# A two-layer attention encoder: swapped rotary halves by DMA, a sink column in the scores, and another order of output tiles

## The chip, the cores and the metric

The kernel runs on one core of one Trainium2 chip. A core has TensorE (PE, which multiplies matrices into PSUM), VectorE (DVE), ScalarE (ACT), GpSimd (POOL) and SyncE (SP, which here issues every DMA). The engines run at once, each through its own list of instructions in a fixed order, and wait for each other by semaphores. The metric is the time of one execution on the device in microseconds (us).

## The reference: what is computed

An input of 1024 tokens by 1024 features passes two layers and a last RMS normalisation. All is float32.

```python
def even_layer(x, mem_n, table, norm_g, w_in, sink, q_norm, k_norm, w_mem_kv, w_out):
    h = rmsnorm(x, norm_g)
    aq, ak, av, bq, bk, bv, xq, gate = _split(h @ w_in, EVEN_SPLITS)
    y_a = windowed_gqa_sink(heads(aq, A_HEADS), heads(ak, A_KV_HEADS), heads(av, A_KV_HEADS), sink, table)
    cos, sin = axial_rope_tables(S)
    qb = apply_axial_rope(rmsnorm(heads(bq, B_HEADS), q_norm), cos, sin)
    kb = apply_axial_rope(rmsnorm(heads(bk, B_KV_HEADS), k_norm), cos, sin)
    y_b = dense_gqa_blocked(qb, kb, heads(bv, B_KV_HEADS))
    y_x = memory_cross_attention(heads(xq, X_HEADS), mem_n, w_mem_kv)
    y = jnp.concatenate([...y_a, y_b, y_x...], axis=-1) * jax.nn.silu(gate)
    return x + y @ w_out
```

Group A (6 heads of 64) looks at a band of 128 keys to each side. Its softmax has one column more than it has keys, the head's sink logit, which takes a share of the sum and has no value: `softmax(concatenate([logits, sink_col]))[..., :-1]`. Group B (6 heads) looks at all 1024 keys; its queries and keys are normalised by head and rotated: each pair of quarters (x1, x2) becomes (x1 cos - x2 sin, x1 sin + x2 cos). Group X attends to 256 memory tokens. Layer 1 has a differential attention (two softmaxes, one subtracted) in place of A and B, and the same cross-attention, gate and output projection.

## The kernel before, in words

**Precision and matmuls.** Every float32 product is made of three TensorE products: both factors are split in a rounded part and a remainder (suffixes h and l, by a cast and a subtraction), and hi*hi, hi*lo and lo*hi are added up in PSUM (lines 297 and 660).

**Jobs and steps.** A layer is a list of steps (one block of 128 queries, or two, of one head) and a list of jobs (one projection of 128 features for 1024 tokens, in two halves of 512 tokens). `run_steps` emits step by step: the scores of step i and its softmax (`s1`, `finish`), the copy of the finished probabilities into a float32r tile `er` by DMA (`hop`, lines 523 to 529), some steps later their transposes through TensorE (`s2`, line 540) and the products with the values (`s3`). Between them `jobs.pull` emits groups of eight products of the job that is due, so that TensorE has other work while softmaxes run. A scheduler then puts the instructions of each engine in their final order by its own estimate of the times; an edit in one place therefore moves instructions in many others.

**PSUM.** There are two tiles of 1024 columns (tag S, for scores, and for most tiles of the output projection), two of 512 (tag A: `acc` of the projections, `ox`, `ob`, `oa` of the value products, `pre`) and two of 512 (tag T, for transposes). A tile is given out again when what reads it is done.

**The rotated projections** (`rope_job`, bq0 to bq2 and bk, each in two halves). ACT squares `acc` into `sq` (line 778), writes `qg`, scaled by the gain (779), and the two swapped halves of `rot` straight from `acc` (781). DVE multiplies `qg` by cosT and `rot` by sinT (783, 784). One group of eight products later `d1` sums the squares by TensorE (791), makes the variance (794) and adds `qg` and `rot` (796). Features are stored so that the two partners of a rotation lie 64 partitions apart. These jobs run among the eight X steps and the first B steps, from about 90 us on.

**A and B steps** of layer 0 are mixed in the order BBABBABBABBABBAA. A B step takes the row minimum of the negated scores (DVE, 1059), multiplies it by the query's scale (`mr`, DVE, 1063) and takes the exponential with its row sum on ACT (1064). An A step treats two query blocks: DVE adds bias and mask and takes the minimum, with the sink as start value (1132); ACT takes the exponential (1136) and that of the sink (`es`, 1139); DVE adds it to the sum (1141) and takes the reciprocal (1143); POOL scales (1149).

**The output projection** (`out_proj`, once a layer) treats eight tiles of 128 tokens in the order `ORD`. Some tiles had their first 4 or 6 of 8 rounds done before, as fillers (`PRE`: in layer 0 tiles 2 to 5 four rounds, 6 and 7 six; in layer 1 tiles 2, 3 and 4 six). A round is three products for each of two column halves. Tiles 0 and 1 begin with their first 6 (layer 1: 7) rounds, before the last gate is ready. After a tile's products DVE adds the residual (1274), ACT squares and sums (1275), DVE and POOL make the scale (1283, 229), DVE scales (1295), and in layer 0 TensorE transposes the tile (344) for layer 1's projections, one tile behind. `pieces` chooses the PSUM tiles: all but the last take an S tile, and the last two A tiles (in layer 1 one A tile and pieces).

Of the kernel before, what the change touches and what calls it, by code (L numbers as in the profile page):

```python
# [13 lines left out]
F32R = mybir.dt.float32r  # L14
# [18 lines left out]
FAST = ("m0", "m1", "m2", "m3")  # L33
ORD = ((0, 1, 2, 3, 4, 5, 6, 7), (0, 1, 4, 2, 5, 3, 6, 7))
JORD = "xq0 m0 g6 m1 m2 g7 m3 bk bq0 bv bq1 g3 bq2 ak av aq0 g0 aq1 g4 g1 aq2 g5 g2".split()
# [120 lines left out]
def encoder_kernel(ctx, tc, A):  # L156
# [615 lines left out]
    def rope_job(p, dst):  # L772
        gcol = gq if p is not None else small[:, C_KN:C_KN + 1]

        def consume(c0, n, acc):
# [4 lines left out]
            for a, b in ((slice(0, 64), slice(64, 128)), (slice(64, 128), slice(0, 64))):  # L780
                nc.scalar.activation(rot[a, :], acc[b, :], AF.Identity, scale=gcol[b, :])
            cs = slice(c0, c0 + 512)
            nc.vector.tensor_tensor(out=qg, in0=qg, in1=cosT[:, cs], op=ALU.mult)
            nc.vector.tensor_tensor(out=rot, in0=rot, in1=sinT[:, cs], op=ALU.mult)
            st = {}

            def d1():
                T = ps_t("ssq")
                with after_fill():
                    for i in range(4):  # L790
# [3 lines left out]
                nc.vector.tensor_scalar(out=v, in0=T[:, 0:8], scalar1=1.0 / 64, scalar2=EPS,  # L794
                                        op0=ALU.mult, op1=ALU.add)
                nc.vector.tensor_tensor(out=qg, in0=qg, in1=rot, op=ALU.add)
                if p is not None:
# [236 lines left out]
    if True:  # L1034
        def b_step(h, qb):
# [8 lines left out]
            def s1(h=h, qb=qb, e=e):  # L1044
# [17 lines left out]
                mr = stat("mr")  # L1062
                nc.vector.tensor_tensor(out=mr, in0=mn, in1=rq[:, qb, h:h + 1], op=ALU.mult)  # L1063
                nc.scalar.activation(et, Sp, AF.Exp, bias=mr, scale=nrq[:, qb, h:h + 1], accum_out=z)  # L1064
# [44 lines left out]
    if True:  # L1109
        def a_step(h, p):  # L1110
# [5 lines left out]
            def s1(h=h, p=p, e=e):  # L1116
# [5 lines left out]
                Sp = ps_s("sa").rearrange("p (j c) -> p j c", j=2)  # L1122
                et = new_e(M)[:, :768].rearrange("p (j c) -> p j c", j=2)
                mn = stat("mn2", 2)
                z = stat("z2", 2)
                for j in range(2):
                    qb = 2 * p + j
                    lo, hi = max(0, qb - 1) * P, min(8, qb + 2) * P
                    c = lo - (qb - 1) * P
                    n = hi - lo  # L1130
                    qk(Sp[:, j, c:c + n], Aq[h], qb * P, Ak["k"][h // 3], Ak["kl"][h // 3], lo, n)
                    nc.vector.tensor_tensor_reduce(out=et[:, j, c:c + n], in0=Sp[:, j, c:c + n],
                                                   in1=abias[h][:, c:c + n], scale=1.0,
                                                   scalar=nsink[:, h:h + 1], op0=ALU.add, op1=ALU.min,
                                                   accum_out=mn[:, j:j + 1])
                    nc.scalar.activation(et[:, j, c:c + n], et[:, j, c:c + n], AF.Exp,
                                         bias=mn[:, j:j + 1], scale=-1.0, accum_out=z[:, j:j + 1])
                es = stat("es", 2)
                nc.scalar.activation(es, mn, AF.Exp, bias=sinkb[:, h:h + 1], scale=1.0)
                def finish():  # L1140
                    nc.vector.tensor_tensor(out=z, in0=z, in1=es, op=ALU.add)
                    rz = stat("rz2", 2)
# [11 lines left out]
            def hop(p=p, e=e):  # L1154
                t = M.at.tile([P, 1024], F32R, tag="er", name="er", bufs=M.cfg["er"])[:, :768]
                a, b = (P if p == 0 else 0), (768 - P if p == 3 else 768)
                ef = e[0].rearrange("p j c -> p (j c)")
# [58 lines left out]
    def out_proj(l, hT_next, stack):  # L1216
# [12 lines left out]

        def pieces(i):  # L1230
            if i < TT - 1:
                S2 = ps_s("po")
# [355 lines left out]
```

## Time and profile before

| | |
|---|---|
| median of 3 runs | 1253.75 us (1253.59 to 1255.1) |
| the profiled execution | 1255.58 us |
| its span, first to last instruction | 1253.8 us |
| mean granted TensorE clock | 0.996 |
| busy: PE, DVE, ACT, POOL | 1205.5, 817.1, 640.2, 413.5 us |
| DMA | 199.90 MB, 96252 packets on one queue, 47.4% of 16 engines |

A row of a group of instructions gives line, engine, operation, what it writes and reads, shapes and count; then busy us, mean ns of one, and the engine's idle time just before, with what ended it. A row of waits reads "engine, tile and line waiting <- what ended the wait: us in total, times, longest". A row in order of time gives start, length, engine, line, operation and, in brackets, the idle time before. A row of a stage gives its bounds and length, each engine's busy time with its instructions, the granted clock, the DMA share and GB/s. A row of DMA issues gives count, KB each and the median us from issue to landing.

Roughly, input and first projections take the first 60 us; X steps with the rotated projections come until 150 us, the B and A steps until 535, layer 0's output projection until 600, and layer 1 the rest, with its output projection from 1180 us.

### The profile page before, as it was taken

The numbers are of one execution on the slowest core, as the hardware profiler recorded it, in microseconds if no ns is written. First come the engines' busy times: TensorE is split into PE (matmuls) and PEld (weight loads), VectorE is DVE, ScalarE is ACT, GpSimd is POOL, SyncE is SP. The second block draws the span as 40 slices with busy tenths as digits, with TensorE's granted clock in tenths as the row PEclk, the third lists the DMA queues.
The fourth block names the chain that finished last, engine by engine and source line by source line (L and its number), as shares of the span: only waits on it lengthen the run. The fifth ranks groups of instructions, "written<-read, shape, count | busy, mean of one in ns | idle before, by whom it ended". The sixth has DMA issues, their size and how long they took to land. (4 is left out here: it accounts for less than half of the span.)

```text
span 1253.8 us, 19637 instructions
## 1 busy us (share of the span) xinstructions
PE 1205.5 (96%) x6806; PEld 999.2 (80%) x6806; DVE 817.1 (65%) x1545; ACT 640.2 (51%) x1395; POOL 413.5 (33%) x390
## 2 busy tenths in 40 slices
PE   5999999999998999998999999999999999999997
PEld 4887788888887787887888778788887878877876
DVE  5547666377778788746355865766667666678444
ACT  6249654256666766533157644444444454456322
POOL 5023456266666565403122212212122131223100
PEclk9999999999999999999999999999999999999999
DMA  6654444545365575466644334243342433445363
GB/s 252 198 187 149 155 168 150 171 155 201 148 224 191 210 246 186 154 203 213 185 163 144 125 107 120 93 143 108 105 137 76 136 115 118 144 151 189 129 211 118
DMA packets 96350, 199.90 MB, mean 159 GB/s; under 512 B 11478, under 2 KB 31190, under 8 KB 96252
## 3 DMA queue, kind: packets, MB, share of 16 engines
q1 hardware_dynamic: 96252, 198.65, 47.4%
q8 instruction: 54, 0.88, 0.3%
q14 instruction: 44, 0.36, 0.1%
HBM read 79.32 MB, written 31.47 MB: 88 GB/s over the span
## 5 line engine op out<-in xcount | busy, mean ns | idle before, releaser
L297 PE MATMUL acc<-h,wh 128*128 128x512 f32 x1536 | 499.1, 399 | 7.3 <-DVE yt L624 3.1
L297 PEld LDWEIGHTS acc<-h,wh 128*128 128x128 f32 x1536 | 283.2, 188 | 73.3 <-issue 13.4
L297 PE MATMUL acc<-h,wl 128*128 128x512 f32 x768 | 304.6, 397 | 1.8 <-POOL wl L241 1.8
L241 POOL TENSOR_TENSOR wl<-wr,wh 128x512 fp32r<-128x512 f32 x96 | 124.9, 1302 | 340.0 <-DVE wh L239 125.2
L316 DVE TENSOR_TENSOR PTl<-te,PTh 128x512 fp32r<-128x512 f32 x224 | 148.2, 687 | 131.2 <-ACT PTh L315 128.4
L1440 ACT ACTIVATE e<-e,mn 128x1024 f32<-128x1024 f32 x96 | 110.2, 1149 | 130.7 <-DVE mn L1437 127.5
L297 PEld LDWEIGHTS acc<-h,wl 128*128 128x128 f32 x768 | 144.8, 189 | 35.5 <-issue 4.4
L315 ACT CAST PTh<-te 128x512 fp32r<-128x512 f32 x224 | 124.9, 591 | 30.2 <-PE te L540 24.6
L1068 POOL TENSOR_TENSOR e<-e,rz 128x1024 f32<-128x1024 f32 x48 | 91.7, 1913 | 78.1 <-DVE rz L1067 66.7
L1437 DVE CUSTOM_DVE_ANT_0 e<-sc,toep 128x1024 f32<-128x1024 f32 x96 | 113.9, 1217 | 5.3 <-PE sc L1431 5.0
L540 PEld LDWEIGHTS te<-identr,er 128*128 128x128 f32 x896 | 91.8, 143 | 21.1 <-issue 4.1
L540 PE MATMUL te<-identr,er 128*128 128x128 f32 x896 | 100.0, 246 | 7.5 <-issue 3.2
L239 DVE CAST wh<-wr 128x512 fp32r<-128x512 f32 x112 | 59.1, 530 | 43.9 <-PE acc L297 14.4
L1064 ACT ACTIVATE e<-sb,mr,nrq 128x1024 f32<-128x1024 f32 x48 | 58.0, 1208 | 48.4 <-DVE mr L1063 33.9
L1449 DVE SCALAR_TENSOR_TENSOR e<-e,mr 128x1024 f32<-128x1024 f32 x48 | 76.2, 1588 | 1.3
L1464 PE MATMUL oc<-PTh,v 128*128 128x256 f32 x384 | 74.8, 288 | 0.3 <-DVE ckl L1333 0.3
L660 PE MATMUL po<-woh,yh 128*128 128x512 f32 (+1 forms) x172 | 65.9, 383 | 1.5 <-DVE x L1274 1.5
L660 PE MATMUL po<-woh,yl 128*128 128x512 f32 (+1 forms) x172 | 65.6, 381 | 0.0
L660 PE MATMUL po<-wol,yh 128*128 128x512 f32 (+1 forms) x172 | 65.5, 381 | 0.0
L1464 PEld LDWEIGHTS oc<-PTh,v 128*128 128x128 f32 x384 | 61.5, 192 | 0.7 <-DVE ckl L1333 0.6
L1059 DVE TENSOR_REDUCE mn<-sb 128x1 f32<-128x1024 f32 x48 | 58.4, 1216 | 5.1 <-PE sb L509 4.7
L318 ACT ACTIVATE yh<-yr 128x256 fp32r<-128x256 f32 (+2 forms) x56 | 24.0, 448 | 67.3 <-DMA yr<-ysc 38.5
(199 smaller groups left out, 2247.1 us busy)
## 6 DMA issues: line engine op xcount, KB each, us to landing
er<-e SPq DMA_DIRECT2D x112, 512.0 KB, 2.9
wr<-in_w_in SPq DMA_DIRECT2D x96, 256.0 KB, 2.8
ysc<-gy SPq DMA_DIRECT2D x16, 512.0 KB, 2.9
wor<-in_w_out SPq DMA_DIRECT2D x32, 256.0 KB, 3.5
cq<-sg SPq DMA_DIRECT2D x64, 128.0 KB, 2.6
ck<-sg SPq DMA_DIRECT2D x48, 128.0 KB, 2.3
er<-e SPq DMA_DIRECT2D x12, 384.0 KB, 2.8
xpsc<-xh SPq DMA_DIRECT2D x18, 256.0 KB, 2.5
```

The lines of the kernel that those rows point to most:

```text
L239: nc.vector.tensor_copy(hi, raw)
L241: (nc.vector if fast else nc.gpsimd).tensor_tensor(out=lo, in0=raw, in1=hi, op=ALU.subtract)
L297: lastmm[0] = nc.tensor.matmul(acc, a, b[:, k, c0:c0 + n], start=(i == 0), stop=(i == 23))
L315: nc.scalar.copy(hi, src)
L316: return nc.vector.tensor_tensor(out=lo, in0=src, in1=hi, op=ALU.subtract)
L540: nc.tensor.transpose(to[:, i * P:(i + 1) * P], e[0][:, k * P:(k + 1) * P], idt)
L660: lastmm[0] = nc.tensor.matmul(acc, a, b, start=(start and n == 0), stop=(stop and n == 2))
L1068: nc.gpsimd.tensor_tensor(out=et, in0=et, in1=rz.to_broadcast([P, 1024]), op=ALU.mult)
L1437: nc.vector.tensor_tensor_reduce(out=et, in0=Sp, in1=toeps[h][:, w0:w0 + 1024], scale=1.0, scalar=BIG, op0=ALU.add, op1=ALU.min, accum_out ...
L1440: nc.scalar.activation(et, et, AF.Exp, bias=mn[:, m:m + 1], scale=-1.0, accum_out=z[:, m:m + 1])
L1449: nc.vector.scalar_tensor_tensor(out=es[0], in0=es[1], scalar=c, in1=es[0], op0=ALU.mult, op1=ALU.add)
L1464: nc.tensor.matmul(acc, V[:, kt, v, :], pt[:, kt, :], start=(n == 0), stop=(n == 23))
```

## The change

1. **Rotation.** `rot` is filled by two DMAs from `qg` (the scaled tile) and no longer by two ACT instructions from `acc`. The products with cosT and sinT move into `d1`, behind the variance.
2. **B steps.** `mr` is made by ACT and no longer by DVE.
3. **Sink.** The score tile of an A step is one column wider for each of its two blocks (a pitch of 385 in place of 384), and ACT copies the negated sink logit into that column: one copy of two columns for three of four steps, two copies of one for the last. The exponential covers it, so that its row sum holds the sink's share; `es` and the addition to `z` go. The copy to `er` covers 769 or 641 columns in place of 768 or 640. Transposes and scaling read the same elements as before, the second block's from an offset of 385.
4. **Output tiles.** `ORD` changes in both layers, and the third tile takes two A tiles in place of an S tile, so that its residual, squares and scaling come in two halves.

In instructions: ACT loses 16 copies of 64x512 and 24 `es`, and gains 48 `mr` and 30 copies of one or two columns; DVE loses 48 `mr` and 24 additions; SP gains 16 DMAs of 64x512 for the rotation and two more for output pieces. TensorE's products are the same.

The scheduler's order differs from about the first rotated projection on. Three places. First DVE, at the second half of bq0 among the X steps (`yt` are the sums that read the value products `ox`, `mn` is the row minimum of an X step, `v` the variance). Before:

```order
L596 RECIPROCAL rz_1473<-z_1385 128x4
L794 TENSOR_SCALAR v_1427<-ssq 128x8
L783 TENSOR_TENSOR qg<-qg,cosT 128x512
L587 TENSOR_REDUCE mn_1513<-sx 128x4
L784 TENSOR_TENSOR rot<-rot,sinT 128x512
L624 TENSOR_TENSOR yt<-ox,yt 64x256 x2
L796 TENSOR_TENSOR qg<-qg,rot 128x512
L624 TENSOR_TENSOR yt<-ox,yt 64x256 x2
```

and now:

```order
L596 RECIPROCAL rz_1473<-z_1385 128x4
L587 TENSOR_REDUCE mn_1513<-sx 128x4
L624 TENSOR_TENSOR yt<-ox,yt 64x256 x2
L596 RECIPROCAL rz_1555<-z_1516 128x4
L624 TENSOR_TENSOR yt<-ox,yt 64x256 x2
L794 TENSOR_TENSOR qg<-qg,cosT 128x512
L795 TENSOR_TENSOR rot<-rot,sinT 128x512
```

Both pairs of `yt` now stand ahead of the table products, which here belong to bq0's first half, and the minimum still stands ahead of them.

Second ACT, at an A step between two B steps (`te` and `ta` are transposed probabilities). Before:

```order
L1064 ACTIVATE e,z<-sb,mr,nrq 128x1024
L315 CAST PTh<-te 128x4x128 x2
L1136 ACTIVATE e,z_2976<-e,mn_2975 128x384 x2
L1139 ACTIVATE es<-mn_2975,small 128x2
L437 COPY yt<-ob 64x256
```

and now:

```order
L1063 ACTIVATE mr<-mn,rq 128x1
L315 CAST PTh<-te 128x4x128
L1064 ACTIVATE e,z<-sb,mr,nrq 128x1024
L315 CAST PTh<-te 128x4x128
L1128 COPY e<-nsink 128x2
L1142 ACTIVATE e,z_2972<-e,mn_2971 128x385 x2
L437 COPY yt<-ob 64x256
```

`mr` and the sink's copy have come in, `es` has gone, and the second exponential is followed by `yt` at once.

Third DVE, in layer 1's output projection, at the third tile (`x` is the tile with its residual, `xs` the scaled one, `yl` the remainder of a later tile's gated input). Before:

```order
L1295 SCALAR_TENSOR_TENSOR xs<-x_13081,r,gb 128x1024
L1283 TENSOR_SCALAR v<-z_13111 128x1
L319 SCALAR_TENSOR_TENSOR yl<-yr,yh 128x128 x2
L1295 SCALAR_TENSOR_TENSOR xs<-x_13109,r,gb 128x1024
L1274 TENSOR_TENSOR x_13153<-po,xr 128x1024
L319 SCALAR_TENSOR_TENSOR yl<-yr,yh 128x128
L1274 TENSOR_TENSOR x_13188<-po,xr 128x1024
```

and now:

```order
L1301 SCALAR_TENSOR_TENSOR xs<-x_13054,r,gb 128x1024
L1289 TENSOR_SCALAR v<-z_13084 128x1
L1301 SCALAR_TENSOR_TENSOR xs<-x_13082,r,gb 128x1024
L1280 TENSOR_TENSOR x_13163<-po,xr 128x512
L319 SCALAR_TENSOR_TENSOR yl<-yr,yh 128x256
L319 SCALAR_TENSOR_TENSOR yl<-yr,yh 128x128 x2
L1280 TENSOR_TENSOR x_13163<-po,xr 128x512
```

The third tile's sum, one instruction after both scalings before, is now two halves with the next tiles' remainders between.

```diff
-ORD = ((0, 1, 2, 3, 4, 5, 6, 7), (0, 1, 4, 2, 5, 3, 6, 7))
+ORD = ((0, 1, 2, 6, 3, 7, 4, 5), (0, 1, 5, 2, 6, 3, 4, 7))
...
             nc.scalar.activation(qg, acc, AF.Identity, scale=gcol)
             for a, b in ((slice(0, 64), slice(64, 128)), (slice(64, 128), slice(0, 64))):
-                nc.scalar.activation(rot[a, :], acc[b, :], AF.Identity, scale=gcol[b, :])
+                dma(rot[a, :], qg[b, :])
             cs = slice(c0, c0 + 512)
-            nc.vector.tensor_tensor(out=qg, in0=qg, in1=cosT[:, cs], op=ALU.mult)
-            nc.vector.tensor_tensor(out=rot, in0=rot, in1=sinT[:, cs], op=ALU.mult)
...
                 nc.vector.tensor_scalar(out=v, in0=T[:, 0:8], scalar1=1.0 / 64, scalar2=EPS,
                                         op0=ALU.mult, op1=ALU.add)
+                nc.vector.tensor_tensor(out=qg, in0=qg, in1=cosT[:, cs], op=ALU.mult)
+                nc.vector.tensor_tensor(out=rot, in0=rot, in1=sinT[:, cs], op=ALU.mult)
                 nc.vector.tensor_tensor(out=qg, in0=qg, in1=rot, op=ALU.add)
...
-                nc.vector.tensor_tensor(out=mr, in0=mn, in1=rq[:, qb, h:h + 1], op=ALU.mult)
+                nc.scalar.activation(mr, mn, AF.Identity, scale=rq[:, qb, h:h + 1])
...
-                et = new_e(M)[:, :768].rearrange("p (j c) -> p j c", j=2)
+                et = new_e(M)[:, :770].rearrange("p (j c) -> p j c", j=2)
...
+                ends = [(min(8, qb + 2) - qb + 1) * P for qb in (2 * p, 2 * p + 1)]
+                if ends[0] == ends[1]:
+                    nc.scalar.copy(et[:, :, ends[0]], nsink[:, h:h + 1].to_broadcast([P, 2]))
+                else:
+                    for j in range(2):
+                        nc.scalar.copy(et[:, j, ends[j]:ends[j] + 1], nsink[:, h:h + 1])
...
-                    nc.scalar.activation(et[:, j, c:c + n], et[:, j, c:c + n], AF.Exp,
+                    nc.scalar.activation(et[:, j, c:c + n + 1], et[:, j, c:c + n + 1], AF.Exp,
                                          bias=mn[:, j:j + 1], scale=-1.0, accum_out=z[:, j:j + 1])
-                es = stat("es", 2)
-                nc.scalar.activation(es, mn, AF.Exp, bias=sinkb[:, h:h + 1], scale=1.0)
                 def finish():
-                    nc.vector.tensor_tensor(out=z, in0=z, in1=es, op=ALU.add)
...
-                t = M.at.tile([P, 1024], F32R, tag="er", name="er", bufs=M.cfg["er"])[:, :768]
-                a, b = (P if p == 0 else 0), (768 - P if p == 3 else 768)
+                t = M.at.tile([P, 1024], F32R, tag="er", name="er", bufs=M.cfg["er"])[:, :770]
+                a, b = (P if p == 0 else 0), (769 - P if p == 3 else 769)
...
         def pieces(i):
+            if i == 2:
+                p = [(ps_a("po")[:, 0:512], c, 512) for c in (0, 512)]
+                return p, p
```

## The prediction

> **What bounds the kernel now.** I read the table of busy time first, to see which engine sets the end; then busy time by stage, to see where that engine still rests; then its waits in those stages; and last, in order of time, the engines that it waited for.
>
> ```profile
> span 1253.8 us, 19637 instructions
> PE 1205.5 (96%) x6806; PEld 999.2 (80%) x6806; DVE 817.1 (65%) x1545; ACT 640.2 (51%) x1395; POOL 413.5 (33%) x390
> ```
>
> TensorE (PE) is busy 1205.5 of 1253.8 us, the next engine 817. The change removes no product that the result needs, so all it can win is time in which PE rests or runs slowly. The busy time by stage shows where (after the stage's bounds and length stand the busy us of PE, PEld, DVE, ACT and POOL, then the granted clock):
>
> ```profile
> 90.00:150.00 60.00, 55.12 (x324) 46.51 (x322) 38.38 (x68) 48.89 (x125) 21.89 (x19) 0.97 0.47 154
> 100.00:125.00 25.00, 23.64 (x148) 20.27 (x147) 18.61 (x33) 24.65 (x68) 9.33 (x9) 1.00 0.56 164
> 250.00:510.00 260.00, 249.57 (x1540) 212.87 (x1538) 202.65 (x448) 170.77 (x380) 160.93 (x144) 0.99 0.55 194
> 540.00:600.00 60.00, 55.97 (x276) 45.57 (x275) 37.01 (x59) 21.84 (x45) 13.19 (x16) 1.00 0.67 212
> 860.00:960.00 100.00, 100.00 (x567) 80.86 (x567) 68.73 (x121) 48.62 (x97) 21.60 (x22) 1.00 0.33 108
> ```
>
> The last row is the middle of layer 1, which the change leaves alone: PE does not rest there. The other stages are those it touches: the rotated projections among the cross-attention steps (4.9 us of PE's rest in 60; ACT is full, 24.65 of 25 us, in the second row), the mixed A and B steps of layer 0 (10.4 in 260) and layer 0's output projection with the hand-over to layer 1 (4.0 in 60). PE's own waits there, and around layer 1's output projection, by who ended them:
>
> ```profile
> PE acc L297 <- DVE yt L624: 3.1, 2, 1.8
> PE ssq L791 <- DVE PTl L316: 1.1, 1, 1.1
> ...
> PE te L540 <- issue: 3.2, 5, 1.4
> PE sa L509 <- ACT e L1064: 2.1, 2, 1.1
> PE sa L509 <- DVE mn L1132: 1.7, 3, 1.1
> PE pre L660 <- DVE yt L438: 1.2, 1, 1.2
> PE ob L1081 <- DVE PTl L316: 0.6, 3, 0.3
> ...
> PE tx L344 <- DVE h L316: 1.7, 1, 1.7
> PE tx L344 <- DVE xs L1295: 1.2, 2, 0.7
> PE acc L297 <- DVE v L1283: 1.1, 1, 1.1
> ...
> PE po L660 <- DVE x L1274: 1.5, 1, 1.5
> ```
>
> These rows hold 4.2, 8.8, 4.0 and 1.5 us. They are many short waits, 18.5 us in all, so the whole prize is near one and a half per cent. Twice a wait is followed by slow PE time:
>
> ```profile
> 128.00:130.80 2.80, 0.98 (x9) 0.80 (x7) 2.75 (x5) 2.73 (x8) 1.96 (x3) 1.00 0.36 132
> 130.83:134.24 3.41, 3.41 (x9) 2.64 (x10) 3.26 (x6) 3.22 (x11) 1.81 (x2) 0.50 0.20 77
> 426.00:431.20 5.20, 2.96 (x12) 1.91 (x11) 2.98 (x5) 4.14 (x8) 2.10 (x2) 1.00 0.81 277
> 431.21:434.60 3.39, 3.39 (x15) 2.80 (x14) 2.86 (x7) 2.58 (x6) 1.75 (x2) 0.50 0.69 233
> ```
>
> For 3.41 us the granted clock is 0.50, at once after PE had rested 1.8 us of 2.8 and 2.2 of 5.2. Half the clock for 3.41 us costs 1.7 us each time.
>
> **The rotated projections.** Sixteen ACT copies of 64x512 go, sixteen DMAs come, and the two table products move behind the statistics' product.
>
> ```profile
> L781 ACT ACTIVATE rot<-acc,misc 64x512 f32<-64x512 f32 x12 | 8.2, 683 | 0.2
> ...
> 126.87 0.68 DVE L783 TENSOR_TENSOR qg<-qg,cosT 128x512 f32<-128x512 f32 x1
> 128.01 1.23 DVE L587 TENSOR_REDUCE mn<-sx 128x4 f32<-128x1024 f32 x1 [0.46 <-PE sx L509]
> 129.15 0.68 DVE L784 TENSOR_TENSOR rot<-rot,sinT 128x512 f32<-128x512 f32 x1
> 129.74 0.85 DVE L624 TENSOR_TENSOR yt<-ox,yt 64x256 f32<-64x256 f32 x2
> ```
>
> ACT loses 16 x 0.683 = 10.9 us, 1.37 for each half projection, in the stage in which it is full, and each accumulator of a rotated projection is released that much earlier. The last rows are the DVE's side of the longest wait (1.8 us): the sums yt that release a bank stand behind both table products. In the new order, shown with the change, they stand ahead of them but still behind the row minimum, 1.23 us. So of the 3.1 us I take 1.9 off, of the 1.1 us 0.6, and half of the 1.7 us of slow clock, 0.9: together 3.4. Both ends: 0 off, or all, 4.2 + 1.7 = 5.9.
>
> Against it stands a new wait. The product with cosT overwrites what the DMAs read and the one with sinT reads what they write, so the DVE waits for two landings in line, and behind it stand yt, the weights' casts and the row minima. The nearest rows: a swap of the same 128 KB, another copy between tiles, the time of one issue, and what SP stood for longest:
>
> ```profile
> cq<-sg SPq DMA_DIRECT2D x64, 128.0 KB, 2.6
> er<-e SPq DMA_DIRECT2D x12, 384.0 KB, 2.8
> ...
> 531.61 0.32 SPq L175 DMA_DIRECT2D xpsc<-xh  x1
> ...
> SPq L175 <- POOL wl L241: 164.8, 69, 6.7
> ```
>
> The landing of 128 KB takes 2.6 us; with 0.32 for the second issue it is there 2.9 us after the scaling, when SP is free. In the new DVE order six of the eight places have 2.5 us or more of work ahead of the products (minima of 1.2, casts and differences of 0.4 to 0.7). The bq1 projection's first half has about 1.6, with one yt pair behind it: 1.3 us late. Twice the swap stands behind a weight load on SP, which then waits a mean 164.8/69 = 2.4 us for POOL. I take 1.3 us for all of it; ends 0 and 8 x 1.3 = 10.4. The stage: 3.4 - 1.3 = **2.1 us won**.
>
> **The A and B steps.** The sink becomes a column of the scores, so the exponential's own sum holds it; the addition and the extra exponential go, and the product mr of the B steps moves from DVE to ACT.
>
> ```profile
> L1063 DVE TENSOR_TENSOR mr<-mn,rq 128x1 f32<-128x1 f32 x48 | 9.3, 193 | 0.7
> L1141 DVE TENSOR_TENSOR z<-z,es 128x2 f32<-128x2 f32 x24 | 6.9, 286 | 14.0 <-ACT es L1139 13.9
> L1139 ACT ACTIVATE es<-mn,small 128x2 f32<-128x2 f32 x24 | 6.8, 281 | 0.0
> L1483 ACT ACTIVATE z<-ssqc,es 128x1 f32<-128x1 f32 x48 | 10.0, 258 | 4.5 <-PE ssqc L1479 4.3
> L1064 ACT ACTIVATE e<-sb,mr,nrq 128x1024 f32<-128x1024 f32 x48 | 58.0, 1208 | 48.4 <-DVE mr L1063 33.9
> ```
>
> DVE is freed of 9.3 + 6.9 us and of 14.0 us in which it stood in line for es: 30 us, nearly all between 150 and 510 us. ACT pays 48 x 0.26 (row L1483, the nearest of one column) = 12.4 and 30 copies of one or two columns at 0.26 to 0.28 = 8, less 6.8: 13.6 us more. Its cover is the 48.4 us in which it idles before the B exponential, 1.0 us a step against 0.26; if that were gone, all 12.4 us would be on the path. One element more per row in the exponentials and four bytes more in the copies of the scores are below what these rows resolve; the second block's odd pitch I cost at 0: what it could lengthen first is the copy to er (384 KB in 2.8 us, above), which is issued two steps before its transposes; were it 1 us longer in all 24 steps and nothing hid it, that would be 24 us, and nothing in the trace is near that.
>
> Of PE's waits here 3.5 us are on DVE (mn, yt, PTl) and 2.1 on ACT; the 3.2 us under "issue" I leave. With a tenth more free time on DVE I take off half of the DVE part, 1.75, and half of the slow clock, 0.85; ACT's share may rise, and I give 0.2 back: **2.4 us won**. Ends: all of it, 3.5 + 2.1 + 1.7 = 7.3 won, or 12.4 lost.
>
> On the clock there is a rule. The Trainium skill (TensorE: Matmul & The Clock Gate, Part 1) has the clock halved after an idle window of about 3.4 us. The waits of this trace are 1.8 and 2.2 us, so by the page neither would cause it and the 1.75 us that I count would stay. Yet in both places the half clock starts with PE's return, and I go by the rows; by the page the sum below would be 1.75 us less.
>
> **Layer 0's output projection.** The short tiles 6 and 7, with two of eight rounds left, move from the end to between long ones, and the third tile takes the A banks.
>
> ```profile
> 560.36 1.23 DVE L1274 TENSOR_TENSOR x<-po,xr 128x1024 f32<-128x1024 f32 x1
> 564.06 1.28 DVE L1295 SCALAR_TENSOR_TENSOR xs<-x,r,gb 128x1024 f32<-128x1024 f32 x1 [0.66 <-POOL r L229]
> 580.26 0.48 PE L660 MATMUL po<-woh,yh 128*128 128x512 f32 x1
> 583.53 0.39 PE L660 MATMUL po<-woh,yl 128*128 128x512 f32 x1
> ```
>
> A tile's vector chain takes 564.06 + 1.28 - 560.36 = 5.0 us; fifteen products start within 583.53 - 580.26 = 3.27 us, 0.23 each. Before, two short tiles follow each other and 4.0 us of waits pile up at the hand-over. After, each chain has a short tile, two or three products and the transposes of another tile (0.8 us) as cover, 4.0 to 4.2 us: waits of some 0.3 (third tile, whose halves overlap), 1.0 and, at the end, 0.7. So 4.0 becomes 2.0: **2.0 us won**; ends 4.0 won and 2.0 lost.
>
> **Layer 1's output projection.** The 1.5 us wait is the fifth tile's for the third's bank. With the third in the A banks the fifth takes the second's, read out some 11 us (48 products of 0.23) earlier. **1.5 us won**; ends 0 and 1.5. The last tile and what follows it are as before.
>
> **Sum.** 2.1 + 2.4 + 2.0 + 1.5 = 8.0 us. The profiled execution took 1255.58 us, with 1.8 us around its span of 1253.8; less 8.0 it is 1247.6. The median of the runs shown is 1253.75, 1.83 lower, so the forecast is 1245.75, and the forecast's own range is 1241 to 1250.
>
> **Rivals.** *The waits only change place* (0.18). For it: the order of instructions on every engine of layer 0 differs from about 90 us on, and PE's waits are short ones that any order makes. Then only layer 1's 1.5 us and half of layer 0's 2.0 stay: 1251.5 to 1254, no change that can be told. Against it: ACT's full stretch and DVE's 14 us in line are removed and not moved.
>
> *The landing of the swap decides* (0.12), the other side. SP serves its queue in order; if at each of the eight swaps it first stands 2.4 us for POOL at a weight load, as twice now, the landing is 2.9 + 2.4 = 5.3 us after the scaling. DVE then stands 2.8 us in six places and 3.7 in two, 24 us, with the sums that release PE's banks behind it. DVE rests a third of that stage (38.38 of 60 us busy), so I pass half of it, 12 us, to PE: 8.0 + 1.3 - 12 = 2.7 us lost, and with a quarter more passed on, 15 us, 5.7 lost: 1256.5 to 1259.5. It decides from 9.3 us passed on. Against it: only two swaps stand behind a weight load.
>
> *More goes than I take* (0.12): all of the first stage's and both output projections' waits and 4.0 of the 7.3 us of the A and B steps: 5.9 + 4.0 + 4.0 + 1.5 = 15.4 us: 1238.
>
> **How the numbers follow.** My forecast has 0.58. A difference under 0.2%, 2.5 us, cannot be told from none in this kernel. Faster: 0.58 + 0.12 and 0.01 of the first rival, 0.71. Within 0.2%: the other 0.17 of the first rival and 0.01 of the second, 0.18. Slower: the rest of the second, 0.11. The range 1238 to 1254 leaves out the slower cases and the last of the large gain.
>
> **What would show it.** Right: ACT below 24 of 25 us around 100 to 125, no DVE time before z of the A steps, the granted clock 1.00 around 130 us, no PE wait on x in layer 1's output projection. Wrong: a DVE wait of over 3 us in all for a DMA at the product with cosT; PE waits on ACT in the A and B steps above 4 us; or PE's rest in 250 to 510 us still above 10 us.

## The result, and the profile after

The changed kernel takes 1259.07 us (median of 6, 1258.33 to 1263.13) against 1252.99 us of the kernel before on the same chips (median of 6). The ratio is 1.0056 with a 95% interval of 1.0038 to 1.0074: about 7 us slower by the ratio, 6.1 by the medians. The forecast was 1245.75 us, with a range of 1238 to 1254.

The page's table of busy time, changed kernel:

```profile
PE 1205.2 (96%) x6806; PEld 1000.6 (80%) x6806; DVE 815.2 (65%) x1479; ACT 639.9 (51%) x1437; POOL 411.3 (33%) x390
```

The profiled execution took 1258.6 us, 3.0 more than that of before. Its span is 1256.8 us against 1253.8. PE does the same work, 1205.2 us busy against 1205.5, so by this table the 3.0 us more are rest of PE. The busy time by stage, in the order of the prediction's rows, changed kernel:

```profile
90.00:150.00 60.00, 52.51 (x306) 44.66 (x305) 37.01 (x60) 39.88 (x109) 18.86 (x16) 0.94 0.45 146
100.00:125.00 25.00, 23.26 (x152) 19.99 (x150) 17.09 (x30) 19.70 (x55) 9.34 (x9) 1.00 0.54 174
150.00:250.00 100.00, 97.01 (x510) 80.74 (x509) 56.71 (x86) 38.50 (x74) 46.32 (x36) 1.00 0.49 160
250.00:510.00 260.00, 249.66 (x1550) 215.48 (x1549) 196.78 (x392) 178.18 (x424) 160.83 (x143) 0.99 0.56 201
```

Between 90 and 150 us PE rests 7.5 us, before 4.9, and the granted clock is 0.94, before 0.97. ACT is busy 39.9 of 60 us, before 48.9, and between 100 and 125 us, where it had been full, 19.7 of 25: the relief came, and PE got nothing from it. Between 150 and 250 us PE rests 3.0 us, where it had rested 0.2; the row before:

```profile
150.00:250.00 100.00, 99.84 (x533) 84.43 (x534) 56.66 (x100) 42.25 (x76) 48.46 (x38) 1.00 0.48 157
```

PE's waits in these two stages, changed kernel, in this order:

```profile
PE ox L616 <- DVE yt L624: 2.2, 1, 2.2
PE acc L297 <- DVE yt L624: 1.9, 1, 1.9
PE tv L405 <- ACT vraw L400: 1.8, 1, 1.8
PE rbc L815 <- ACT rr L808: 1.1, 1, 1.1
PE te L540 <- DVE rot L816: 0.4, 1, 0.4
...
PE acc L297 <- DVE yt L624: 1.5, 2, 1.2
PE ob L1081 <- DVE gy L426: 0.8, 1, 0.8
PE sb L509 <- DMA q<-bq_d: 0.6, 1, 0.6
```

That is 7.4 and 2.9 us; before it was 4.5 and 0.4. The half clock that follows a rest now lasts 6.83 us:

```profile
123.72:127.13 3.41, 1.24 (x11) 1.06 (x10) 2.33 (x5) 3.35 (x12) 1.46 (x2) 1.00 0.71 193
127.13:133.96 6.83, 4.90 (x15) 4.02 (x16) 3.55 (x6) 4.53 (x16) 1.79 (x2) 0.50 0.46 155
```

**The sum of a rotated half comes late.** For the first half of bq0, the ACT rows of the kernel before, scaling and then the cast of the finished sum:

```profile
117.67 0.70 ACT L779 ACTIVATE qg<-acc,misc 128x512 f32<-128x512 f32 x1
...
121.57 0.62 ACT L315 CAST sg<-qg 128x512 fp32r<-128x512 f32 x1
```

The same half in the changed kernel, with SP's and DVE's rows between, in order of time:

```profile
118.57 0.67 ACT L779 ACTIVATE qg<-acc,misc 128x512 f32<-128x512 f32 x1
...
123.17 1.23 SPq L175 DMA_DIRECT2D bkl<-sg  x2
124.50 1.18 SPq L175 DMA_DIRECT2D rot<-qg  x2
...
129.90 0.86 DVE L624 TENSOR_TENSOR yt<-ox,yt 64x256 f32<-64x256 f32 x2 [1.04 <-ACT yt L621]
130.78 0.69 DVE L794 TENSOR_TENSOR qg<-qg,cosT 128x512 f32<-128x512 f32 x1
131.40 1.23 DVE L795 TENSOR_TENSOR rot<-rot,sinT 128x512 f32<-128x512 f32 x1
132.65 0.69 DVE L796 TENSOR_TENSOR qg<-qg,rot 128x512 f32<-128x512 f32 x1
133.38 0.62 ACT L315 CAST sg<-qg 128x512 fp32r<-128x512 f32 x1 [1.84 <-DVE qg L796]
```

From the end of the scaling to the cast it took 3.2 us (121.57 - 118.37) and takes 14.1 (133.38 - 119.24). For 5.3 us SP serves the keys' copies, which stand ahead of the swap; two issues take 1.2 us, the landing 2.5 (its median). By then, about 128.2, DVE's list has sums `yt` ahead of the products, which start 2.6 us later, and the three operations take 2.6 us. Who stands at the end of that chain is ACT, which reaches the cast and waits, with the squares, scalings and copies that release PE's banks behind it. ACT's and DVE's waits between 90 and 220 us, changed kernel:

```profile
ACT sg L315 <- DVE qg L796: 11.3, 5, 5.4
DVE qg L794 <- DMA rot<-qg: 0.6, 1, 0.6
```

and ACT's wait at that cast before:

```profile
ACT sg L315 <- DVE qg L796: 1.4, 3, 1.0
```

DVE, of which I expected the wait, stands 0.6 us in all for a landing; ACT stands 11.3 where it had stood 1.4. In one place the stand can be followed to PE. ACT stands 5.42 us at the cast, the copy `vraw` is next in its list, and the 1.8 us that PE waits on `vraw` (above) end with that copy:

```profile
146.56 0.62 ACT L315 CAST sg<-qg 128x512 fp32r<-128x512 f32 x1 [5.42 <-DVE qg L796]
147.09 0.58 ACT L400 COPY vraw<-acc 128x512 f32<-128x512 f32 x1
```

Not all of PE's rest can be laid to this. The two longest waits, 2.2 and 1.9 us on the sums `yt`, end at 127.02 and here:

```profile
130.90 1.19 PE L297 MATMUL acc<-h,wh 128*128 128x512 f32 x2 [1.93 <-DVE yt L624]
```

Both are over before ACT first stands at this cast, from 131.54 to 133.38. Before, PE waited for `yt` as well, 3.1 us. Why it is longer now, by late sums or by the new order of the instructions, is not shown.

### The profile page after: what moved, and what is told of

It is laid out like the page before. It is cut to its first block, busy times and chain, and to the rows that moved or that the text cites. A ratio compares the mean times of both kernels' runs of the same rounds, so it can differ in the third digit from the quotient of the medians.

```text
span 1256.8 us, 19688 instructions
## 1 busy us (share of the span) xinstructions
PE 1205.2 (96%) x6806; PEld 1000.6 (80%) x6806; DVE 815.2 (65%) x1479; ACT 639.9 (51%) x1437; POOL 411.3 (33%) x390
```

## The experiments

All times were taken in five rounds against the kernel before on the same chip; us are the ratio times the kernel before.

### The four parts alone

The rotated projections' edit alone:

```diff
-                nc.scalar.activation(rot[a, :], acc[b, :], AF.Identity, scale=gcol[b, :])
+                dma(rot[a, :], qg[b, :])
...
-            nc.vector.tensor_tensor(out=qg, in0=qg, in1=cosT[:, cs], op=ALU.mult)
-            nc.vector.tensor_tensor(out=rot, in0=rot, in1=sinT[:, cs], op=ALU.mult)
...
+                nc.vector.tensor_tensor(out=qg, in0=qg, in1=cosT[:, cs], op=ALU.mult)
+                nc.vector.tensor_tensor(out=rot, in0=rot, in1=sinT[:, cs], op=ALU.mult)
```

> The kernel before with the rotated projections' edit alone (swapped halves by DMA, both table products behind the statistics' product). Theory A, the edit itself costs: the sums of the changed kernel's trace put its loss into 90 to 250 us, where PE waits 7.4 + 2.9 us by the waits against 4.5 + 0.4 before and the half clock grows from 3.4 to 6.8 us (1.7 us of time): 5.4 + 1.7 = 7.1 us lost there. Then this kernel alone is 5 to 8 us slower than before (1.004 to 1.0065). Theory B, only the order of all the changed parts together costs: within 2.5 us of before. Theory C, the prediction's term: 2.1 us faster.

Measured: 1264.69 us, 1.0084 [1.0069, 1.0099], 10.5 us slower. The whole loss of the change is here, and more. Its stages, 90 to 150 and 150 to 250 us:

```profile
90.00:150.00 60.00, 52.12 (x299) 44.10 (x298) 36.31 (x59) 38.92 (x107) 18.88 (x16) 0.94 0.44 143
150.00:250.00 100.00, 96.17 (x497) 79.69 (x497) 59.09 (x94) 35.88 (x67) 45.97 (x36) 0.98 0.48 158
```

PE rests 7.9 and 3.8 us there against 4.9 and 0.2, 6.6 more, and the clock of 0.94 and 0.98 adds at most 3.4. Theory A stands; it was priced 2.5 us too low at its upper end.

The product mr on ACT alone:

```diff
-                nc.vector.tensor_tensor(out=mr, in0=mn, in1=rq[:, qb, h:h + 1], op=ALU.mult)
+                nc.scalar.activation(mr, mn, AF.Identity, scale=rq[:, qb, h:h + 1])
```

> The kernel before with the product mr of the B steps on ACT alone. By the prediction part of its 2.4 us of the A and B steps, so 0 to 2 us faster. Rival: ACT's 48 small operations delay its copies of the transposes, as the two waits on ACT (2.3 and 1.9 us) between 405 and 460 us of the changed kernel suggest: 2 to 4 us slower.

Measured: 1252.13 us, 0.9985 [0.9974, 0.9996], 1.9 us faster, at the upper end of what the prediction gave it. The rival's wait is there too, and does not outweigh the gain:

```profile
PE ob L1081 <- ACT PTh L315: 2.6, 1, 2.6
```

The sink column alone (pitch of 385, a copy of the sink, one exponential):

```diff
+                if ends[0] == ends[1]:
+                    nc.scalar.copy(et[:, :, ends[0]], nsink[:, h:h + 1].to_broadcast([P, 2]))
...
-                nc.scalar.activation(es, mn, AF.Exp, bias=sinkb[:, h:h + 1], scale=1.0)
...
-                    nc.vector.tensor_tensor(out=z, in0=z, in1=es, op=ALU.add)
```

> The kernel before with the sink column alone. By the prediction 0.5 to 2.4 us faster, since DVE no longer stands 14 us for es. Rival: the copies of the sink stand on ACT ahead of the score's exponential, and the odd pitch slows what reads the scores: 2 to 4 us slower, with PE waits on ACT above 3 us between 250 and 510 us.

Measured: 1254.21 us, 1.0005 [0.9993, 1.0017]: no difference, below what either expected. DVE's 14 us in line for `es` were no wait of PE, and most of them did not go. DVE now waits for the exponential itself, one step later, at the reciprocal:

```profile
DVE rz L1146 <- ACT e L1142: 10.8, 17, 0.8
```

PE's waits on ACT between 250 and 510 us sum to 4.0 us, above the 3 of the rival, and yet the time stays.

Both tile orders and the third tile alone:

```diff
-ORD = ((0, 1, 2, 3, 4, 5, 6, 7), (0, 1, 4, 2, 5, 3, 6, 7))
+ORD = ((0, 1, 2, 6, 3, 7, 4, 5), (0, 1, 5, 2, 6, 3, 4, 7))
...
+            if i == 2:
+                p = [(ps_a("po")[:, 0:512], c, 512) for c in (0, 512)]
+                return p, p
```

> The kernel before with both new tile orders and the third tile in the A banks alone. By the changed kernel's trace layer 1's wait of 1.5 us is gone and layer 0's waits fall from 4.0 to 2.8 us: 1.5 to 3 us faster. By the prediction 3.5 us faster. Rival, that layer 0's order only moves its waits: 1.5 us faster, all of it after 1110 us.

Measured: 1252.34 us, 0.9986 [0.9973, 0.9999], 1.8 us faster. Layer 1's wait of 1.5 us on x is gone. Layer 0's waits between 540 and 600 us were 4.0 and are one row:

```profile
PE tx L344 <- DVE xs L1298: 3.1, 5, 1.2
```

So layer 0 gave about 1 us of the 2.0. The 1.8 us lie in the 1.5 to 3 read from the changed kernel's trace; the rival's 1.5 is nearer than the prediction's 3.5.

### All but the rotated projections' edit

```diff
-                dma(rot[a, :], qg[b, :])
+                nc.scalar.activation(rot[a, :], acc[b, :], AF.Identity, scale=gcol[b, :])
```

with both products back in their old place.

> The changed kernel with the rotated projections' edit undone: swapped halves copied by ACT and table products ahead of the statistics, the rest (product mr on ACT, sink column, tile orders, third tile) as changed. If the parts add up, 1.9 + 1.7 - 0.5 = 3.1 us faster than before, 1251. If the sink column or the order of the A and B steps costs more in company, as the 0.5 + 0.3 us of new waits on ACT between 405 and 460 us could mean, no change. And against the changed kernel about 8 to 10 us faster, if its loss is the swap alone.

Measured: 1247.82 us, 0.9955 [0.9939, 0.9971], 5.6 us faster than before. The profile's stages 90 to 150 and 250 to 510 us:

```profile
90.00:150.00 60.00, 56.22 (x338) 47.84 (x337) 39.03 (x70) 49.56 (x127) 23.54 (x19) 1.00 0.50 163
...
250.00:510.00 260.00, 249.31 (x1563) 214.56 (x1562) 198.60 (x396) 181.04 (x431) 164.44 (x147) 1.00 0.56 199
```

That is more than the 3.1 us that the parts alone add up to. PE rests 10.7 us in the A and B steps, as much as before, but the granted clock is 1.00 in both stages: in this execution no rest before the last products was followed by half a clock. Against the changed kernel it is 1.0056 - 0.9955 = 1.0%, 12.7 us: the loss is the rotated projections' edit alone.

### What in the swap costs

Later products with ACT's copies kept:

```diff
-            nc.vector.tensor_tensor(out=qg, in0=qg, in1=cosT[:, cs], op=ALU.mult)
-            nc.vector.tensor_tensor(out=rot, in0=rot, in1=sinT[:, cs], op=ALU.mult)
...
+                nc.vector.tensor_tensor(out=qg, in0=qg, in1=cosT[:, cs], op=ALU.mult)
+                nc.vector.tensor_tensor(out=rot, in0=rot, in1=sinT[:, cs], op=ALU.mult)
```

> The kernel before with the two table products behind the statistics' product, but with ACT's copies of the swapped halves kept, so without any new DMA. Theory A1 (it is the DMA's way that makes the sum late, its place in SP's queue and its landing): within 2.5 us of before. Theory A2 (it is the later place of the products in DVE's order): slower by 5 to 10 us, like the whole edit's 10.5 us.

Measured: 1250.79 us, 0.9984 [0.9971, 0.9996]. 2.0 us faster, just clear of noise. PE rests 3.1 us in the stage, and ACT waits for the sums no longer than before:

```profile
90.00:150.00 60.00, 56.86 (x341) 48.07 (x340) 39.58 (x71) 49.42 (x126) 22.90 (x19) 1.00 0.48 158
ACT sg L315 <- DVE qg L796: 1.5, 3, 1.0
```

The place in the text is later, but the order that runs hardly is. DVE's order, by operations and tile names, differs from that of before at 28 of 1545 places, and bq0's first product with cosT still starts at 118.23 us, 0.03 after its scaling. So this run does not show what products that truly stand later would cost, and A2 is not tested by it.

The DMAs with the products in their old place:

```diff
-                nc.scalar.activation(rot[a, :], acc[b, :], AF.Identity, scale=gcol[b, :])
+                dma(rot[a, :], qg[b, :])
```

> The kernel before with the swapped halves by DMA and both table products left ahead of the statistics' product. Theory A1: slower by 6 to 12 us, and DVE now stands before the products for the landing, eight times 2 to 9 us between 90 and 220 us. Theory A2: within 2.5 us of before, since the products keep their place in DVE's order.

Measured: 1265.48 us, 1.0094 [1.0074, 1.0113], 11.8 us slower. The wait that A1 expected of DVE is not there:

```profile
ACT sg L315 <- DVE qg L796: 17.0, 5, 5.5
DVE qg L783 <- DMA rot<-qg: 0.9, 2, 0.7
```

DVE stands 0.9 us, ACT 17.0. The products stand ahead of the statistics in the text, yet the order of operations and tiles in this trace is that of the first experiment (the edit alone) on every engine. So this run is the first experiment again, and the two agree (1.0084 and 1.0094). It shows that the place in the text does not matter once the DMAs are there: the scheduler puts the products late either way. It does not tell A1 from A2, the landing from the late place in DVE's order.

A second buffer for the scaled tile, the edit else as in the first experiment and the order the same on all engines:

```diff
-            qg, rot = (top.tile([P, 512], F32, tag=n_, name=n_, bufs=1) for n_ in ("qg", "rot"))
+            qg, rot = (top.tile([P, 512], F32, tag=n_, name=n_, bufs=b_) for n_, b_ in (("qg", 2), ("rot", 1)))
```

> The rotated projections' edit alone (1.0084 of before), with a second buffer for the scaled tile; the order of the instructions on all five engines is the same as in that kernel. In its trace the time from scaling to sum is 6.5 to 13 us against 3 to 5.4 before, and three of eight scalings start within 0.05 us after the casts of the half before them. Theory A3 (the single buffer makes the accumulator wait for the half before): 4 to 8 us of the 10.5 come back. Theory A4 (only the fixed order with its late sums costs, the buffer is no matter): less than 2 us comes back.

Measured: 1264.68 us, 1.0089 [1.0072, 1.0106]. Nothing comes back, A3 falls. ACT's rows show why:

```profile
133.84 0.62 ACT L315 CAST sg<-qg 128x512 fp32r<-128x512 f32 x1 [1.84 <-DVE qg L796]
...
134.85 0.68 ACT L779 ACTIVATE qg<-acc,misc 128x512 f32<-128x512 f32 x1
```

The next scaling stands behind the cast in ACT's own list, so a free buffer is of no use to it.

Another queue for the swap, first ACT's, then POOL's:

```diff
-                dma(rot[a, :], qg[b, :])
+                dma(rot[a, :], qg[b, :], nc.scalar)
```

> The rotated projections' edit alone, with the sixteen swap DMAs issued from ACT, at once behind the scaling, and no longer from SP. In the changed kernel's trace the first swap of a pair is issued 0.0, 4.1, 5.3, 1.2, 1.2, 2.2, 0.0 and 1.7 us after the scaling ended, 15.7 us in all, since SP serves the weight loads and the keys' copies ahead of it. Theory S (SP's line makes the sums late): 5 to 10 of the 10.5 us come back, 1254 to 1259. Theory L (issue and landing themselves, 1.2 + 2.5 us for each pair, make them late): less than 4 us comes back, 1260 or more.

Measured: 1261.03 us, 1.0069 [1.0055, 1.0083], 8.6 us slower; 1.9 of 10.5 us come back, as theory L expected.

> The same edit with the swap DMAs issued from POOL, which has fewer DMAs ahead but splits the weights (1.3 us for one 128x512 part). Theory S: some 3 to 8 us come back, as far as POOL is free when the scaling ends. Theory L: less than 4 us comes back, or, where POOL's issue delays the weights' low parts, slower than with SP.

Measured (`nc.gpsimd` in that line): 1259.03 us, 1.005 [1.0037, 1.0062], 6.3 us slower; 4.2 us come back, inside theory S's 3 to 8 and just past theory L's bound. So SP's line costs a part: moving the issue gives 2 to 4 us, net of what the other queue loses by it. The rest stays when the issue follows the scaling at once. In the kernel with ACT's queue the first issue starts 0.03 us after the scaling in seven of eight halves, and the sum is still finished only 6.9 to 9.0 us after the scaling, where it was 3.0 to 5.4 before. Its waits:

```profile
ACT sg L315 <- DVE qg L796: 20.4, 6, 5.0
DVE qg L794 <- DMA rot<-qg: 5.4, 4, 2.8
```

Now DVE does stand for the landing, 5.4 us, and ACT still waits for the sums, 20.4. PE waits 3.4 us for the squares (line 778), which stand behind such casts in ACT's list, and with POOL's queue 5.5 us.

No swap at all, neither copies nor DMAs:

```diff
-            for a, b in ((slice(0, 64), slice(64, 128)), (slice(64, 128), slice(0, 64))):
-                nc.scalar.activation(rot[a, :], acc[b, :], AF.Identity, scale=gcol[b, :])
...
+                nc.vector.tensor_tensor(out=rot, in0=qg, in1=sinT[:, cs], op=ALU.mult)
+                nc.vector.tensor_tensor(out=qg, in0=qg, in1=cosT[:, cs], op=ALU.mult)
```

> The kernel before with the swap of the halves left out (the product with sinT reads the scaled tile itself, so the rotated projections are another function): no ACT copies, no DMAs, both products behind the statistics. It bounds what freeing ACT of 10.9 us can bring. By the prediction 3.4 us of this stage, so 1249 to 1251 with the later products' 2.0 us partly in it; rival, ACT's copies are not what PE waits for: within 1 us of the kernel with later products and ACT's copies, 1250 to 1252.

Measured: 1249.83 us, 0.9971 [0.9961, 0.9982], 3.6 us faster, within the prediction's 1249 to 1251. The later products gave 2.0 of them, which leaves about 1.6 for ACT's relief itself; the two intervals overlap, so that part is not shown. In the stage PE rests 1.5 us:

```profile
90.00:150.00 60.00, 58.47 (x351) 49.27 (x350) 38.82 (x72) 44.61 (x117) 22.95 (x19) 1.00 0.50 163
```

The same DMAs, but nothing reads what they write:

```diff
-                dma(rot[a, :], qg[b, :])
+                dma(aside[a, :], qg[b, :])
...
-                nc.vector.tensor_tensor(out=qg, in0=qg, in1=cosT[:, cs], op=ALU.mult)
+                nc.vector.tensor_tensor(out=rot, in0=qg, in1=cosT[:, cs], op=ALU.mult)
...
-                nc.vector.tensor_tensor(out=qg, in0=qg, in1=rot, op=ALU.add)
+                nc.vector.tensor_tensor(out=rot, in0=qg, in1=rot, op=ALU.add)
```

> The rotated projections' edit alone, but the swap DMAs write a tile that nothing reads, and the table products read the scaled tile alone (so the rotated projections are another function; as many DMAs, products and bytes as before). Theory W (the sums wait for issue and landing, and that costs): it runs like the kernel without any swap, 1.00 - 0.003, so 1249 to 1252. Theory Q (the DMAs in SP's queue delay the loads and copies behind them): it stays at 1.007 to 1.0085 of before, 1261 to 1264.

Measured: 1251.67 us, 0.9989 [0.9976, 1.0001], 1.4 us faster. The stages and the tile's landing times:

```profile
90.00:150.00 60.00, 57.96 (x346) 49.04 (x345) 39.64 (x72) 44.27 (x118) 21.81 (x19) 1.00 0.55 172
150.00:250.00 100.00, 99.62 (x544) 84.58 (x543) 55.16 (x102) 38.85 (x74) 49.86 (x39) 1.00 0.52 174
...
DMA to landing us min/median/max: 2.2/2.9/5.6
```

Sixteen DMAs of the same size run through the same queue, and PE rests 2.0 and 0.4 us, not 7.9 and 3.8. Theory W stands: 1.0084 - 0.9989 = 0.95%, 11.9 us, is the price of sums that wait for a landing. The DMAs' presence may cost some 2.2 us, the difference to the kernel without a swap; those two intervals overlap. The scheduler ordered this kernel anew as well, with the products close behind the scaling, so the 11.9 us hold both the waits and the order that it builds around them; these two were not separated. But four different orders wait for all the landings (the changed kernel, the edit alone, ACT's and POOL's queue), and all are slower.

Swap by DMA for the key projection's two halves only:

```diff
+                if p is None:
+                    dma(rot[a, :], qg[b, :])
+                else:
+                    nc.scalar.activation(rot[a, :], acc[b, :], AF.Identity, scale=gcol[b, :])
```

> Later table products, and swap DMAs only for the two halves of the key projection; the six halves of the query projections keep ACT's copies. Theory W with an equal cost for each sum that is late: of the 12.5 us between later products with copies (0.9984) and with DMAs (1.0084) a quarter, 3 us: 1.0005 to 1.002. If the keys' halves, among the cross-attention steps where ACT was full, are where it all happens: 6 us or more, 1.003 or more. If the queries' halves are: within 1 us of 0.9984.

Measured: 1256.4 us, 1.002 [1.0011, 1.0029]. Two of eight late sums cost 0.36%, 4.5 us, against later products with copies; eight cost 1.0%, 12.5 us. That is 2.3 us for one against 1.6, at the upper edge of an equal price. But the trace does not show an equal price paid at the cast:

```profile
90.00:150.00 60.00, 55.86 (x311) 47.42 (x310) 35.98 (x64) 43.87 (x116) 18.99 (x16) 0.91 0.48 158
ACT sg L315 <- DVE qg L799: 1.2, 2, 1.0
```

ACT waits there no longer than before, and PE rests 4.1 us, 1.0 more than with copies. What stands out is the clock: it is half from 127.40 to 137.64 us, 10.24 us, where the kernel with copies has none. Over the twelve runs of each the mean granted clock is 0.9942 against 0.9967, which is up to 3.1 us of the 4.5. So here most of the price may be the slow clock after a rest of PE, and what a rest costs depends on where it falls.

### The best of it

The later products kept, ACT's copies back, all else as changed (the first line of the change undone):

```diff
-                dma(rot[a, :], qg[b, :])
+                nc.scalar.activation(rot[a, :], acc[b, :], AF.Identity, scale=gcol[b, :])
```

> The changed kernel with ACT's copies in place of the swap DMAs, all else as changed, the table products behind the statistics included. That edit undone wholly gave 0.9955 of before, and the later products alone 0.9984. If they add up: 0.994, 1246; if the order decides and not the edit: anything from 0.993 to 0.998.

Measured: 1247.57 us, 0.9958 [0.9945, 0.997], 5.3 us faster than before. It beats both kernels, and cannot be told from the one with the products in their old place; the 2.0 us of the later products did not add up. The orders of these two differ little as well, at 19 of DVE's 1479 places.

Without the sink column, and without the rotated projections' edit:

```diff
+                nc.scalar.activation(mr, mn, AF.Identity, scale=rq[:, qb, h:h + 1])
...
+ORD = ((0, 1, 2, 6, 3, 7, 4, 5), (0, 1, 5, 2, 6, 3, 4, 7))
```

> The product mr on ACT, both new tile orders and the third tile in the A banks, without the sink column and without the rotated projections' edit. Alone they gave 0.9985 and 0.9986, in sum 3.6 us won. With the sink column beside them it was 5.7 us. If the sink column wins in company what it did not win alone, this kernel stays at 0.997 to 0.998; if it does nothing, 0.9955.

Measured: 1248.71 us, 0.996 [0.9948, 0.9972], 5.0 us faster: `mr` and the output tiles hold the gain, the sink column adds nothing that can be told. Alone the two gave 3.7 us; whether 5.0 is more than their sum the intervals leave open.

## Why the prediction was wrong

**The rotated projections: the step that failed.** "I take 1.3 us for all of it; ends 0 and 8 x 1.3 = 10.4" was the price of waiting for the landing, against 3.4 us won. The 3.4 were about right in size: 3.6 in the kernel that leaves the swap out, where the later products with ACT's copies kept had given 2.0. The wait cost 11.9 us with the order that the scheduler built around it, nine times the value taken and above the upper end; with the 2.2 us that the DMAs' presence may cost it is 14.1 (10.5 lost in place of 3.6 won). Two errors are behind that. I asked only whether DVE would stand, and credited DVE's other work ahead of the products as cover. It was cover for DVE, which stands 0.6 us. But the sum is late either way, by up to 11 us in the half shown, and ACT waits for it in order with reads that free PE's banks behind. And I put the issue directly behind the scaling, save for two swaps behind a weight load, and took 0.32 us for the second; in fact an issue took 0.59, and the first of each pair stood 0 to 5.3 us behind the scaling, 15.7 in all, longest behind the keys' own copies. How the 11.9 us divide between ACT's stand, the new order and the clock stays open: in the changed kernel's trace only 1.8 of the 7.4 us between 90 and 150 us could be followed from ACT's stand to PE.

**The rival "the landing of the swap decides"** came true in its place and its time (1256.5 to 1259.5), at a chance of 0.12. Its mechanism did not: DVE was to stand 24 us, POOL's weights to hold SP. The engine that stood was ACT, and SP's line is the smaller part. That what it passed on to PE, 12 to 15 us, is near what the wait cost, 11.9 to 14.1, is luck.

**The A and B steps**, 2.4 us won: 1.9 with `mr` alone, none with the sink column. The size holds, the reason only half: DVE's rests of 14 us for `es` were not PE's, and with the sink column 10.8 us of rest stand at the reciprocal (8.6 in the changed kernel). The prediction had held against its first rival that they "are removed and not moved"; in the main they moved.

**The output projections**, 2.0 + 1.5 us won: 1.8 in all. Layer 1's wait went as worked out; layer 0's fell from 4.0 to 3.1 and not to 2.0 us, since PE still waits for each tile's scaled values.

Together these two terms were 5.9 us, and the kernel with them and without the swap won 5.6. Alone their parts give 3.1, so that the two sums agree is in part luck. Still the forecast fails by one term: 5.6 won and 12.7 lost make the 7 us.

**The clock.** I went by the rows and not by the rule of the Trainium skill that the prediction names, and the runs bear the rows out (below). The half clock grew from 6.8 us in all to 13.7 before the last products, which is at most 3.4 us of time. The prediction priced only what the clock would win. The changed kernel's six runs have a mean granted clock of 0.9927, the kernel before 0.9960 to 0.9965 beside the experiments: 0.0033 to 0.0038 of 1257 us, so up to 4 to 5 of the 7 us lost can be slower clock after the new rests.

**The signs.** ACT is at 19.7 of 25 us, no DVE time before z remains (it moved to the reciprocal), PE no longer waits on x in layer 1: right, and without worth for the time in the first two cases. The clock around 130 us is 0.50, not 1.00. Of the signs of failure, PE's waits on ACT in the A and B steps (2.3 + 1.9 us) and PE's rest there (10.3 us) just passed their bounds; the sign at DVE's cosT product did not show, because it looked at the wrong engine.

## What to carry to other kernels

When an engine's copy is replaced by a DMA inside a dependent chain, price the whole way from the last write to the first reader (the queue's line, both issues, the landing, the reader's next free place in its list), and then ask which in-order engine reaches the chain's result first and what it holds behind it. Idle time of that reader is no cover for those who wait behind the result. To test such a thing, let the same DMA run with nothing that reads what it wrote: here it told 11.9 us of waiting, with the order built around it, from some 2 us of traffic. And where a scheduler has the last word, compare the orders that run before two edits are called two experiments.

## What the runs showed of the hardware

**The clock falls after half a window of rest.** The half-clock stretches begin on a grid of 3.413 us: before at 130.83 and 431.21, which is 88 periods apart. How long PE was busy in the stretch ahead goes with it. Two such stretches, the first of the kernel before, the second of the changed kernel:

```profile
127.42:130.83 3.41, 1.59 (x14) 1.41 (x13) 2.91 (x6) 3.33 (x9) 2.57 (x3) 1.00 0.45 153
```

```profile
144.20:147.61 3.41, 1.73 (x8) 1.11 (x6) 2.97 (x4) 1.05 (x2) 1.67 (x2) 1.00 0.23 77
```

With 1.59 us busy the next stretch ran at 0.50; with 1.73 it ran at 1.00. The Trainium skill (TensorE: Matmul & The Clock Gate, Part 1) has a free-running window of 3413 ns, which agrees, and names one idle window as the cause, which does not: a stretch with half of it at rest was enough. The bound is not sharp by PE's busy time as modelled here: in the runs' traces, after their first 15 us, every stretch with less than 1.6 us busy was followed by half a clock, and stretches between 1.6 and 2.2 went both ways. In the kernel with POOL's queue a stretch with 2.13 us busy was followed by half a clock:

```profile
169.56:172.97 3.41, 2.13 (x14) 1.61 (x13) 3.33 (x6) 2.32 (x5) 2.86 (x4) 1.00 0.91 358
172.97:176.38 3.41, 3.41 (x16) 2.72 (x14) 0.87 (x5) 1.65 (x3) 3.30 (x4) 0.50 0.90 291
```

The half clock lasted one, two or, in the kernel with the keys' swaps alone, three periods (10.24 us). The same wait can so cost nothing more, or up to 1.7 us for each period, by where the grid lies in that execution.

**A product on DVE took up to 1.78 us in place of 0.68.** The product with sinT in the changed kernel (all eight; its shortest, median and longest ns), and two rows of one case, DVE's and POOL's:

```profile
L795 DVE TENSOR_TENSOR rot<-rot,sinT x8: 680/685/1780, 98.0 to 215.3; 128x512 f32<-128x512 f32 x8
...
143.96 1.78 DVE L795 TENSOR_TENSOR rot<-rot,sinT 128x512 f32<-128x512 f32 x1
...
143.59 1.61 POOL L241 TENSOR_TENSOR wl<-wr,wh 128x512 fp32r<-128x512 f32 x1 [4.07 <-DVE wh L239]
```

Before, the same eight products took 680 to 692 ns; but two of the products with cosT took 1.00 and 1.80 us, so the delay as such is not new. The Trainium skill (SBUF — State Buffer, "SBUF: two separate sides") lets a DVE operation with two SBUF operands and a reading GpSimd operation exclude each other through a shared port, where the one that starts first holds it to its end. The changed kernel's trace agrees: all six long ones among the products with cosT and sinT started while a POOL operation of 0.91 to 1.91 us was running, and ended 0.54 to 0.56 us after it (here 145.20 and 145.74). Those with 0.68 started before such an operation, or beside none; POOL's operations on 128x8 did not lengthen them. No run here took POOL's work away, so this is a match in time and not an experiment.
